# One layer of a hybrid encoder on one Trainium2 core: attention rounds in one piece, full-height neighbourhood scores, w_ple products moved, norms of the end among products, 80 expert blocks ahead

## The chip, the core and the metric

One core of a Trainium2 chip runs the whole layer. TensorE (PE in the profile) multiplies, VectorE (DVE), ScalarE (ACT) and GpSimd (POOL) do the elementwise work, SyncE (SP) issues most DMAs. The metric is the time of one execution on the device in microseconds; the median of three runs is given.

## The reference

A layer over 512 tokens of width 1024, all in float32. An RMS norm and one projection give queries, keys and values of two attentions and two gates. (A) Neighbourhood attention: 8 heads of 64, every token looks at an 8 x 16 window of a grid of 8 rows and 64 columns, with a learned bias. (B) Dilated attention: 12 heads of 64 in three groups with different windows and strides, whose outputs are mixed by their softmax denominators. The outputs are projected, gated, merged and added to x. Then comes a retrieval of experts:

```
q  = rms_norm(x) @ w_query;  s1, s2 = q_halves @ sub_keys        # 128 keys a side, 8 heads
the 16 best of the sums s1 + s2, softmax weights g               # of 128 x 128 experts
x += sum over (head, k) of  gelu(h . expert_u[e]) * g * expert_v[e]
x += sigmoid(rms_norm(x) @ w_ple_gate) * (p @ w_ple)
```

## The kernel before

**Split products.** A float32 weight block is loaded by SP (`wr`), cast to a high part by ScalarE (`wh`, L141) and its rest taken by VectorE (`wl`, L143; letter `v`) or GpSimd (L149; letter `p`). A product is then three matmuls (L171 to L173). The class `Stream` does this in order of `W.add`: three loads ahead, five split blocks at a time; `take` hands blocks to the products and `free` gives their place to the next. Attention scores, transposes and value products are plain float32; a plain float32 product appears as two passes in the trace, a transpose as one.

**Order of work.** Instructions are written in code order, and a scheduler with its own estimate of durations places them on each engine, so the order on TensorE can differ from the code's. `beside` registers filler (a generator of products), and `tick(dt)` lets it go on for the time dt times its rate.

**Stages.** (1) Projections. (2) `pipeline` (L477) runs dilated attention in 24 items of three steps: scores, transposes (`turn`), value products. In each round it calls the scores of one item, the transposes of the item before and the values of the one before that, with a `tick` after each. The filler is the neighbourhood projection. (3) The same for 32 neighbourhood items (a head of a quarter of the tokens each), filler `gates`. A score is one matmul with 64 rows: head h of a pair lies on partitions 0 to 63 or 64 to 127 of `nqk`. (4) Gated branch products (`p`), then w_out (`xo`); after each token tile's second half `norm_parts` (L748) makes the normed tile, transposes it in bank Q and splits it to `hhi`, `hlo`. (5) Query products (`qp`), key scores (`sk`) and the search of the best 16 on VectorE. (6) `ple` twice: pT and w_ple are loaded, 48 matmuls (`pl`), and the results go by 256 columns through a buffer shared with the Gelu outputs (tag `ge`, three deep) to `ple_d` in memory. (7) Ahead: the 128 expert blocks are worked on by whole blocks of `up` (L1008): 24 matmuls `aT`, then a Gelu. For the first NSP = 76 blocks this runs as filler, and the Gelu outputs are stored to `ge_d`. Beside it VectorE builds G, the gate weights of all experts, by one-hot products (`gp`), staged to memory in six parts (`g_d`). One token tile is treated otherwise: its 256 rows of experts are gathered by GpSimd and summed on VectorE (`experts0`). (8) Fused: the 52 later blocks are computed (`up`) and all 128 multiplied with the second expert table (`down`, 18 matmuls `out`); the stored ones are loaded again (`gr`). Four fresh blocks go before the first loaded group. (9) The last `down` products go token tile by token tile, then four norms (`third`), then the w_ple_gate products (`pg`), the gate and the output.

Of the kernel before, what the change touches and what calls it, by code (L numbers as in the profile page):

```python
# [10 lines left out]
F32 = mybir.dt.float32  # L11
# [19 lines left out]

OB = 2

NSP = 76

RATE_LAST, RATE_HEAD, AHEAD = 0.0, 0.1, 1.0
RATE_G, RATE_GATES, EARLY = 1.45, 0.3, 30.0
# [27 lines left out]
def block_kernel(ctx: ExitStack, tc: tile.TileContext, a: dict):  # L65
# [160 lines left out]
    pT = a["pT"].rearrange("(k p) t -> p k t", p=128)  # L226
    for b in range(2):
        add_block(wo, 512 * b, lo="vp")
    for b in range(4):
        add_block(wq, 512 * b, lo="p" if b else "vp")  # L230
    for b in range(2):
        W.add(pT, 2, "p")
        add_block(wpl, 512 * b, lo="p")


    hhi = hpool.tile([128, 8, S], F32R, name="hhi")
# [126 lines left out]
            return qn  # L363
        return second

    def transpose4(src, name="pt"):

        pt = bank("Q", name)
        for c in range(4):
            nc.tensor.transpose(pt[:, 128 * c:128 * c + 128], src[:, 128 * c:128 * c + 128], ident)  # L370
        return pt.rearrange("p (c t) -> p c t", c=4)
# [63 lines left out]
    dils = ExitStack()  # L435
    dilp = dils.enter_context(tc.tile_pool(name="dilp", bufs=1))
    dqk = [dilp.tile([128, 4, 512], F32, name=f"dqk{b}") for b in range(3)]
    dv = [dilp.tile([128, 4, 512], F32, name=f"dv{b}") for b in range(2)]

    dmask = dils.enter_context(tc.tile_pool(name="dmask", bufs=1))  # L440
    m12 = dmask.tile([128, 4, 128], F32, name="m12")
# [35 lines left out]
    def pipeline(items):  # L477

        n = len(items)
        depth = max(len(x) for x in items)  # L480
        for t in range(n + depth - 1):
            for s in range(depth):
                if 0 <= t - s < n and s < len(items[t - s]):
                    tick(items[t - s][s]() or 0.0)


    nas = ExitStack()
    nap = nas.enter_context(tc.tile_pool(name="nap", bufs=1, side="right"))
    nqk = [nap.tile([128, 4, 512], F32, name=f"nqk{s}") for s in range(2)]
    nv = nap.tile([128, 4, 512], F32, name="nv")  # L490

    def na_qk(s):
        def first(i, ps):
            norm = qk_norm(ps, eps_of("j", i))
            box = []

            def third():
                pt = transpose4(box[0].rearrange("p h d -> p (h d)"))
                nc.scalar.activation(nqk[s][:, :, 128 * i:128 * i + 128], pt, AF.Copy, scale=gna[:, s:s + 1])
            return [(3, lambda: box.append(norm())), (7, third)]  # L500
        return first

# [133 lines left out]
    onalo = afix2.tile([128, 4, 512], F32R, name="onalo")  # L636
    gts = ExitStack()
    gt = gts.enter_context(tc.tile_pool(name="gt", bufs=1)).tile([128, 2, 8, 512], F32, name="gt")
    nabs = ExitStack()
    nabp = nabs.enter_context(tc.tile_pool(name="nabp", bufs=1))  # L640

    last_exp = []

# [7 lines left out]
    def na_items(j):  # L651
# [6 lines left out]
        box = {}  # L658

        def bias(hp):  # L660
            t = box["nab", hp] = nabp.tile([128, 2, 256], F32, tag="nab", name="nab", bufs=2)
            nc.sync.dma_start(t, src[:, 2 * hp:2 * hp + 2])

        def item(h):
            p0 = 64 * (h % 2)

            def scores():
                if h == 0:
                    bias(0)
                if h % 2 == 0 and h < 6:  # L670
                    bias(h // 2 + 1)
                sp = bank("P", "sp")[:, :n]
                nc.tensor.matmul(sp, nqk[0][p0:p0 + 64, h // 2, 128 * j:128 * j + 128],
                                 nqk[1][p0:p0 + 64, h // 2, k0:k0 + n], start=True, stop=True)
                sc = box["sc", h] = wk.tile([128, 512], F32, tag="sc", name="sc", bufs=3)[:, :n]
                nc.vector.scalar_tensor_tensor(sc, sp, 0.125, box["nab", h // 2][:, h % 2], op0=ALU.mult, op1=ALU.add)
                nc.vector.tensor_reduce(nm[:, h:h + 1], sc, AX.X, ALU.max, negate=True)
                last_exp[:] = [nc.scalar.activation(sc, sc, AF.Exp, bias=nm[:, h:h + 1],
                                                    accum_out=sums[:, h:h + 1]).ins]
                return n * 4 / 2400  # L680

            def turn():
                pt = bank("Q", "ptp")[:, :n]
                for c in range(nk):
                    nc.tensor.transpose(pt[:, 128 * c:128 * c + 128], box["sc", h][:, 128 * c:128 * c + 128], ident)
                pT = box["pT", h] = wk.tile([128, 512], F32, tag="pT", name="pT", bufs=2)[:, :n]
                nc.scalar.copy(pT, pt)
                return nk * 0.107

            def values():  # L690
                if "uo" not in box:
                    box["uo"] = bank("C", "uo")
                for c in range(nk):
                    nc.tensor.matmul(box["uo"][:, 64 * h:64 * h + 64], box["pT", h][:, 128 * c:128 * c + 128],
                                     vs[c][:, 64 * h:64 * h + 64], start=(c == 0), stop=(c == nk - 1))
                if h == 7:
                    rs = small.tile([128, 8], F32, tag="nrs", name="nrs")
                    nc.vector.reciprocal(rs, sums)
                    o = nabp.tile([128, 8, 64], F32, tag="no", name="no")
                    nc.vector.tensor_mul(o, box["uo"].rearrange("p (h d) -> p h d", h=8),  # L700
                                         col(rs).to_broadcast([128, 8, 64]))

                    def out():
                        pt = transpose4(o.rearrange("p h d -> p (h d)"))
                        oh = onahi[:, :, 128 * j:128 * j + 128]
                        nc.scalar.copy(oh, pt)
                        nc.vector.tensor_sub(onalo[:, :, 128 * j:128 * j + 128], pt, oh.bitcast(F32))
                        return 0.43
                    outs_later.append(out)
                c = nk * 0.107  # L710
                if h == 1:
                    while outs_later:
                        c += outs_later.pop()()
                return c

            return [scores, turn, values]
# [21 lines left out]
    while outs_later:  # L738
        outs_later.pop()()
    done(s)  # L740
    nabs.close()
    nas.close()
    wks.close()

    def square(src, junk, total):
        nc.scalar.activation(junk, src, AF.Square, accum_out=total)

    def norm_parts(src, gain, hn, ssh, cols):  # L748


        ssn = small.tile([128, 1], F32, tag="ssn", name="ssn")
# [3 lines left out]
        for half in range(2):  # L755
            cs = slice(512 * half, 512 * half + 512)
            nc.vector.scalar_tensor_tensor(hn[:, cs], src[:, cs], r, gain[:, cs], op0=ALU.mult, op1=ALU.mult)
            pt = transpose4(hn[:, cs])
            ks = slice(4 * half, 4 * half + 4)
            nc.scalar.copy(hhi[:, ks, cols], pt)  # L760
            nc.vector.tensor_sub(hlo[:, ks, cols], pt, hhi[:, ks, cols].bitcast(F32))
# [52 lines left out]
    for b in range(2):  # L814
        cols = slice(512 * b, 512 * b + 512)
        units = W.take(4)
        for n in range(4):
# [6 lines left out]
            if b:  # L824
                if n:
                    nc.scalar.dma_start(x2_d[n - 1], y)
                hn = x2p.tile([128, D], F32, tag="hn", name="hn", bufs=2) if n else h2n
                norm_parts(y, gffn, hn, ss2[:, n], ts)
    x2s.close()
    gts.close()  # L830
    at.close()
# [88 lines left out]
    def experts0():  # L920
# [16 lines left out]
        for u, (kind, c) in enumerate(units):  # L937
# [13 lines left out]
                    nc.vector.scalar_tensor_tensor(acc0, t, act0[:, c:c + 1], acc0, op0=ALU.mult, op1=ALU.add)  # L951
            yield 1.0

    tiles0 = select_tiles()
    tqs = ExitStack()
    tq = tqs.enter_context(tc.tile_pool(name="tq", bufs=1))
# [25 lines left out]
    later.pop(0)()  # L982

    tqs.close()


    def ple(b):
        (phi, plo), = W.take(1)
        units = W.take(1)
        for n in range(4):  # L990
            ps = bank("P", "pl")
            ts = slice(128 * n, 128 * n + 128)
            run(cell(ps, lambda k: (phi[:, k, ts], plo[:, k, ts]), units, False))
            for c in range(0, 512, 256):
                po = gel.tile([128, 384], F32, tag="ge", name="po", bufs=3)[:, :256]
                nc.scalar.copy(po, ps[:, c:c + 256])
                nc.sync.dma_start(ple_d[128 * n:128 * n + 128, 512 * b + c:512 * b + c + 256], po)
        W.free()
        W.free()

    ple(0)
    ple(1)


    for b in range(NB):
# [20 lines left out]
    k = 0  # L1026
# [145 lines left out]
            run(down(*pend.pop(0), i - 1, V.take(1)))  # L1172
            V.free()

    units = V.take(len(pend))
    for t in range(3):
        for x, p in enumerate(pend):
            run(down(*p, NB - len(pend) + x, units[x:x + 1], [t]))
    done(exp_side)


    fs = ExitStack()
    fin = fs.enter_context(tc.tile_pool(name="fin", bufs=1))
# [6 lines left out]
        with tc.issue_after(late):  # L1190
            nc.sync.dma_start(x3[n], x2_d[n - 1])

    def third(n):
        hn = fin.tile([128, D], F32, tag="hn", name="hn", bufs=2)
        ss3 = small.tile([128, 2], F32, tag="ss3", name="ss3")
        for h in range(2):
# [1 line left out]
            if n:  # L1198
                nc.vector.tensor_add(x3[n][:, cs], x3[n][:, cs], outs[n - 1][h])
            square(x3[n][:, cs], hn[:, cs], ss3[:, h:h + 1])  # L1200
        norm_parts(x3[n], gple, hn, ss3, slice(128 * n, 128 * n + 128))

    for n in (0, 1, 2, 3):
        third(n)
    for b in range(2):
        cols = slice(512 * b, 512 * b + 512)
        units = W.take(4)
        for n in (0, 1, 2, 3):
            ps = bank("A", "pg")
            ts = slice(128 * n, 128 * n + 128)  # L1210
            run(cell(ps, lambda k: (hhi[:, k, ts], hlo[:, k, ts]), units, n == 3))
            pl = fin.tile([128, 512], F32, tag="pl", name="pl", bufs=2)
            with tc.issue_after(late):
                nc.sync.dma_start(pl, ple_d[128 * n:128 * n + 128, cols])
            sg_ = fin.tile([128, 512], F32, tag="sg", name="sg", bufs=1)
            nc.scalar.activation(sg_, ps, AF.Sigmoid)
            nc.vector.tensor_mul(pl, sg_, pl)
            nc.vector.tensor_add(pl, pl, x3[n][:, cols])
            nc.sync.dma_start(a["out"][128 * n:128 * n + 128, cols], pl)
    fs.close()  # L1220
    dns.close()
    gps.close()
# [66 lines left out]
```

## Time and profile before

| | |
|---|---|
| median of three runs | 1806.03 us (1803.46 to 1808.21) |
| the profiled execution | 1807.68 us, its span 1805.7 us |
| TensorE busy | 1774.1 us |
| VectorE / ScalarE / GpSimd busy | 1314.0 / 727.4 / 525.8 us |
| DMA | 417.11 MB, 231 GB/s in the mean |

Busy time is the union of an engine's instructions. A matmul's busy time contains its filling and draining, which overlap with its neighbours, so a fully busy TensorE can still be slower than its work needs: the distance between the starts of matmuls tells that. "Idle before" names what the engine waited for.

### The profile page before, as it was taken

What the parts mean: (1) busy time and instruction counts of PE and PEld (TensorE: products, weight loads), DVE (VectorE), ACT (ScalarE), POOL (GpSimd) and SP (SyncE); (2) the same over time, 40 slices, a digit from 0 to 9 for tenths busy, and PEclk for the clock granted to TensorE, in tenths of its full rate; (3) what the DMA queues carried; (4) which work ended last, traced back from release to release, by engine and by line L of the source; (5) the groups of instructions that cost most, each with busy time, mean ns of one, the idle gap of its engine ahead of it and who ended that gap; (6) DMA issues with size and microseconds to landing.
All of it is one profiled execution on the core that took longest, in us unless ns stands there. A gap on an engine that the chain in (4) does not pass through costs nothing.

```text
span 1805.7 us, 26185 instructions
## 1 busy us (share of the span) xinstructions
PE 1774.1 (98%) x9613; PEld 1561.1 (86%) x9613; DVE 1314.0 (73%) x2638; ACT 727.4 (40%) x1202; POOL 525.8 (29%) x428
## 2 busy tenths in 40 slices
PE   8999999999899899999999999999999999999998
PEld 7997777788788799999999988888888888888877
DVE  6634644436568899998989578787878878776864
ACT  5434554443323544444444433333333333333342
POOL 4201101113424121223354134343334323333300
PEclk9999999999999999999999999999999999999999
DMA  5231114334312576688888999999999989989922
GB/s 189 77 93 34 47 52 124 96 110 139 118 59 94 164 257 207 242 285 316 305 321 325 365 320 350 341 335 339 342 325 343 351 317 356 343 313 317 347 97 82
DMA packets 159536, 417.11 MB, mean 231 GB/s; under 512 B 14128, under 2 KB 61488, under 8 KB 156336
## 3 DMA queue, kind: packets, MB, share of 16 engines
q1 hardware_dynamic: 122112, 279.64, 44.4%
q0 software_dynamic: 36864, 134.23, 20.8%
q8 instruction: 75, 1.23, 0.3%
q10 hardware_dynamic: 432, 1.57, 0.2%
q14 instruction: 53, 0.43, 0.1%
HBM read 368.73 MB, written 45.88 MB: 230 GB/s over the span
## 4 chain that ended last, share of the span: by engine, by line
PE 91%; DMA 4%; DVE 2%; ACT 1%; issue 1%; SPq 0%; POOL 0%; ACTq 0%; DVEq 0%; POOLq 0%
PE out L1153 27%; PE aT L171 9%; PE aT L173 9%; PE aT L172 9%; PE proj L171 3%; PE proj L172 3%; PE proj L173 3%; PE gp L1103 3%; DMA g_d<-stage 2%; PE gt L173 2%; PE gt L171 2%; PE gt L172 2%; DMA vr<-peer_expert_v 2%; PE qp L171 2%; PE qp L172 2%; PE qp L173 2%
## 5 line engine op out<-in xcount | busy, mean ns | idle before, releaser
L171 PE MATMUL aT<-hhi,wh 128*128 128x384 f32 x1024 | 345.4, 337 | 4.0 <-ACT ge L1020 4.0
L173 PE MATMUL aT<-hhi,wl 128*128 128x384 f32 x1024 | 344.9, 337 | 0.0
L172 PE MATMUL aT<-hlo,wh 128*128 128x384 f32 x1024 | 344.7, 337 | 0.0
L141 ACT CAST wh<-wr 128x1024 fp32r<-128x1024 f32 x216 | 226.8, 1052 | 263.7 <-PE aT L172 194.1
L143 DVE TENSOR_TENSOR wl<-wr,wh 128x1024 fp32r<-128x1024 f32 x184 | 229.0, 1245 | 124.4 <-ACT wh L141 122.9
L932 POOL DMA_INDIRECT gath<-peer_expert_u,eidx x128 | 181.4, 1417 | 435.9 <-DVE gath L943 296.9
L932 POOL DMA_INDIRECT gath<-peer_expert_v,eidx x128 | 191.4, 1495 | 302.3 <-DVE acc L951 213.5
L1153 PE MATMUL out<-vl,ahi 128*128 128x512 f32 x768 | 237.2, 390 | 0.0
L1153 PE MATMUL out<-vh,ahi 128*128 128x512 f32 x768 | 233.0, 391 | 2.4 <-ACT ahi L1141 2.4
L1153 PE MATMUL out<-vh,alo 128*128 128x512 f32 x768 | 233.7, 390 | 0.0
L141 ACT CAST vh<-vr 128x1024 fp32r<-128x1024 f32 x128 | 134.4, 1051 | 178.3 <-DMA vr<-peer_expert_v 156.3
L171 PEld LDWEIGHTS aT<-hhi,wh 128*128 128x128 f32 x1024 | 192.8, 188 | 7.0 <-ACT ge L1020 4.4
L172 PEld LDWEIGHTS aT<-hlo,wh 128*128 128x128 f32 x1024 | 192.9, 188 | 2.3
L173 PEld LDWEIGHTS aT<-hhi,wl 128*128 128x128 f32 x1024 | 192.9, 188 | 1.0
L951 DVE SCALAR_TENSOR_TENSOR acc<-gath,act,acc 128x1024 f32<-128x1024 f32 x128 | 164.0, 1281 | 34.6 <-DMA gath<-peer_expert_v,eidx 34.2
L143 DVE TENSOR_TENSOR vl<-vr,vh 128x1024 fp32r<-128x1024 f32 x128 | 156.1, 1222 | 36.4 <-ACT vh L141 35.1
L149 POOL TENSOR_TENSOR wl<-wr,wh 128x256 fp32r<-128x256 f32 x128 | 99.4, 813 | 250.5 <-ACT wh L141 220.8
L1153 PEld LDWEIGHTS out<-vl,ahi 128*128 128x128 f32 x768 | 144.1, 188 | 31.0 <-DVE vl L143 0.2
L1153 PEld LDWEIGHTS out<-vh,alo 128*128 128x128 f32 x768 | 144.0, 188 | 31.0 <-DVE alo L1143 0.7
L943 DVE SCALAR_TENSOR_TENSOR gath<-gath,h2n 128x1024 f32<-128x1024 f32 x128 | 155.6, 1222 | 20.2 <-DMA gath<-peer_expert_u,eidx 20.0
L1153 PEld LDWEIGHTS out<-vh,ahi 128*128 128x128 f32 x768 | 143.0, 188 | 29.4 <-ACT ahi L1141 3.5
L171 PE MATMUL proj<-wh,hhi 128*128 128x512 f32 (+1 forms) x256 | 108.1, 425 | 6.8 <-ACT wh L141 6.8
(259 smaller groups left out, 2849.2 us busy)
## 6 DMA issues: line engine op xcount, KB each, us to landing
vr<-peer_expert_v SPq DMA_DIRECT2D x128, 512.0 KB
wr<-uT SPq DMA_DIRECT2D x128, 512.0 KB
g_d<-stage SPq DMA_DIRECT2D x24, 1024.0 KB
G<-g_d SPq DMA_DIRECT2D x32, 768.0 KB
wr<-w_in SPq DMA_DIRECT2D x46, 512.0 KB
ge_d<-ge SPq DMA_DIRECT2D x76, 192.0 KB
gr<-ge_d SPq DMA_DIRECT2D x76, 192.0 KB
wr<-peer_w_query SPq DMA_DIRECT2D x16, 512.0 KB
```

Source lines behind the costliest of these rows:

```text
L141: nc.scalar.copy(hi, self.raw[i])
L143: nc.vector.tensor_sub(lo, self.raw[i], hi.bitcast(F32))
L149: nc.gpsimd.tensor_sub(l[:, cs], r[:, cs], h[:, cs].bitcast(F32))
L171: nc.tensor.matmul(ps, st[0], mv[0], start=start, stop=False)
L172: nc.tensor.matmul(ps, st[0], mv[1], start=False, stop=False)
L173: nc.tensor.matmul(ps, st[1], mv[0], start=False, stop=stop)
L932: nc.gpsimd.indirect_dma_start(out=t, out_offset=None, in_=a["peer_expert_" + kind], in_offset=bass.IndirectOffsetOnAxis(ap=eidx[:, c:c + ...
L943: nc.vector.scalar_tensor_tensor(t, t, 1.0, h2n, op0=ALU.mult, op1=ALU.mult, accum_out=a0[:, c:c + 1])
L951: nc.vector.scalar_tensor_tensor(acc0, t, act0[:, c:c + 1], acc0, op0=ALU.mult, op1=ALU.add)
L1103: nc.tensor.matmul(gpb[:, 128 * x:128 * x + 128], o[:, 1, cs], m[:, s, cs], start=(s == 0), stop=(s == 2))
L1153: nc.tensor.matmul(outs[t][h], w[:, cs], x[:, h], start=first and p == 0, stop=last and p == 2)
```

## The change

NSP goes from 76 to 80. `pipeline` calls the three steps of a round and then one `tick` with their sum. Neighbourhood queries are stored by parity of the head into a tensor whose other 64 rows are zero, so that a score multiplies all 128 rows. The bias tiles and outputs of that attention use buffers of the pool `wk`. w_ple products are queued and computed before the query products, and pT is loaded once. `norm_parts` becomes a generator that stops between the normed tile and its transposes; at the end, norms start between the last `down` products, with a bank of their own each, and the transposes stand between the w_ple_gate products, which are in a function `gated` now.

```diff
-NSP = 76
+NSP = 80
...
+    W.add(pT, 2)
+    for b in range(2):
+        add_block(wpl, 512 * b)
     for b in range(4):
         add_block(wq, 512 * b, lo="p" if b else "vp")
-    for b in range(2):
-        W.add(pT, 2, "p")
-        add_block(wpl, 512 * b, lo="p")
...
         for t in range(n + depth - 1):
+            dt = 0.0
             for s in range(depth):
                 if 0 <= t - s < n and s < len(items[t - s]):
-                    tick(items[t - s][s]() or 0.0)
+                    dt += items[t - s][s]() or 0.0
+            tick(dt)
...
-    nqk = [nap.tile([128, 4, 512], F32, name=f"nqk{s}") for s in range(2)]
+    nqz = nap.tile([128, 4, 2, 512], F32, name="nqz")
+    nkk = nap.tile([128, 4, 512], F32, name="nkk")
+    for par in range(2):
+        nc.gpsimd.memset(nqz[64 - 64 * par:128 - 64 * par, :, par], 0.0)
...
-                nc.scalar.activation(nqk[s][:, :, 128 * i:128 * i + 128], pt, AF.Copy, scale=gna[:, s:s + 1])
+                cols = slice(128 * i, 128 * i + 128)
+                if s:
+                    nc.scalar.activation(nkk[:, :, cols], pt, AF.Copy, scale=gna[:, 1:2])
+                    return
+                for par in range(2):
+                    rows = slice(64 * par, 64 * par + 64)
+                    nc.scalar.activation(nqz[rows, :, par, cols], pt[rows], AF.Copy, scale=gna[rows, 0:1])
...
-                nc.tensor.matmul(sp, nqk[0][p0:p0 + 64, h // 2, 128 * j:128 * j + 128],
-                                 nqk[1][p0:p0 + 64, h // 2, k0:k0 + n], start=True, stop=True)
+                nc.tensor.matmul(sp, nqz[:, h // 2, h % 2, 128 * j:128 * j + 128], nkk[:, h // 2, k0:k0 + n],
+                                 start=True, stop=True)
...
-            pt = transpose4(hn[:, cs])
+        yield
+        for half in range(2):
+            pt = transpose4(hn[:, 512 * half:512 * half + 512], tag=tag)
             ks = slice(4 * half, 4 * half + 4)
...
+    (phi, plo), = W.take(1)
+    for b in range(2):
+        units = W.take(1)
+        for n in range(4):
+            ps = bank("P", "pl")
+            ts = slice(128 * n, 128 * n + 128)
+            run(cell(ps, lambda k: (phi[:, k, ts], plo[:, k, ts]), units, False))
+            for c in range(0, 512, 256):
+                po = gel.tile([128, 384], F32, tag="ge", name="po", bufs=3)[:, :256]
+                nc.scalar.copy(po, ps[:, c:c + 256])
+                nc.sync.dma_start(ple_d[128 * n:128 * n + 128, 512 * b + c:512 * b + c + 256], po)
+    for _ in range(3):
+        W.free()
     tiles0 = select_tiles()
...
-    ple(0)
-    ple(1)
...
-    for n in (0, 1, 2, 3):
-        third(n)
+    norms = {}
+    def norm(n):
+        if n in norms:
+            for _ in norms[n]:
+                pass
+            return
         hn = fin.tile([128, D], F32, tag="hn", name="hn", bufs=2)
...
+        norms[n] = norm_parts(x3[n], gple, hn, ss3, slice(128 * n, 128 * n + 128), "APQC"[n])
+        next(norms[n])
...
+    done(exp_side)
+    norm(0)
+    units = V.take(len(pend))
+    for t in range(3):
+        for x, p in enumerate(pend):
+            run(down(*p, NB - len(pend) + x, units[x:x + 1], [t]))
+        if t == 0:
+            norm(0)
+        if t < 2:
+            norm(t + 1)
+    units = W.take(4)
+    gated(0, 0, units)
+    norm(1)
+    norm(3)
+    gated(0, 1, units)
+    norm(2)
+    gated(0, 2, units)
+    norm(3)
+    gated(0, 3, units)
+    units = W.take(4)
+    for n in range(4):
+        gated(1, n, units)
```

## Rows read from the trace of the kernel before

**Rows 1.** The page's first part: busy us, share of the span, instructions.
```profile
PE 1774.1 (98%) x9613; PEld 1561.1 (86%) x9613; DVE 1314.0 (73%) x2638; ACT 727.4 (40%) x1202; POOL 525.8 (29%) x428
```

**Rows 2.** Busy time by stretch: us, engines, granted clock, DMA share, GB/s.
```profile
45.00:480.00 435.00, 434.44 (x2109) 356.65 (x2109) 214.57 (x493) 183.34 (x394) 77.30 (x75) 1.00 0.28 87
595.00:630.00 35.00, 30.10 (x149) 26.70 (x148) 31.54 (x168) 19.58 (x35) 7.01 (x11) 0.95 0.66 207
630.00:1005.00 375.00, 372.77 (x2914) 366.09 (x2913) 342.31 (x578) 172.21 (x278) 118.58 (x58) 1.00 0.79 282
1025.00:1600.00 575.00, 575.00 (x2738) 501.73 (x2737) 462.72 (x608) 210.37 (x288) 214.15 (x168) 1.00 0.95 339
1600.00:1665.00 65.00, 63.10 (x304) 54.82 (x303) 44.92 (x51) 20.58 (x29) 22.78 (x17) 1.00 0.90 318
```

**Rows 3.** Waits of TensorE: us in total, times, longest us.
```profile
PE pt L370 <- DVE hn L757: 4.1, 1, 4.1
PE aT L171 <- ACT ge L1020: 4.0, 1, 4.0
...
PE out L1153 <- ACT ahi L1141: 2.4, 3, 1.1
```

**Rows 4.** Timeline of TensorE in neighbourhood attention: start us, us, instruction.
```profile
297.32 0.39 PE L685 MATMUL ptp<-ident,sc 128*128 128x128 f32 x2
297.64 0.70 PE L673 MATMUL sp<-nqk,nqk 64*128 64x256 f32 x2
298.27 0.50 PE L173 MATMUL gt<-hhi,wl 128*128 128x512 f32 x1
298.61 0.39 PE L171 MATMUL gt<-hhi,wh 128*128 128x512 f32 x1
298.84 0.39 PE L172 MATMUL gt<-hlo,wh 128*128 128x512 f32 x1
```

**Rows 5.** Timeline of TensorE at the sums of squares of the start.
```profile
21.56 0.39 PE L173 MATMUL proj<-wh,hlo 128*128 128x512 f32 x1
21.79 1.88 PE L390 MATMUL ssb<-xsq,ones 128*128 128x512 f32 x4
...
23.97 0.40 PE L172 MATMUL proj<-wl,hhi 128*128 128x512 f32 x1
```

**Rows 6.** Timeline of TensorE where two neighbourhood scores stand together.
```profile
330.60 0.70 PE L673 MATMUL sp<-nqk,nqk 64*128 64x256 f32 x4
...
331.80 0.40 PE L173 MATMUL gt<-hhi,wl 128*128 128x512 f32 x1
```

**Rows 7.** ScalarE's timeline, one exponential's end; then two groups of splits.
```profile
299.78 0.19 ACT L678 ACTIVATION_READ_ACCUMULATOR sc<-sc,nnm 128x1 f32 x1
...
L141 ACT CAST wh<-wr 128x1024 fp32r<-128x1024 f32 x216 | 226.8, 1052 | 263.7 <-PE aT L172 194.1
...
L143 DVE TENSOR_TENSOR wl<-wr,wh 128x1024 fp32r<-128x1024 f32 x79 | 96.6, 1224 | 16.4 <-ACT wh L141 15.8 <-issue 0.6
```

**Rows 8.** Timeline of TensorE from the last w_out product to steady query products.
```profile
485.18 1.03 PE L370 MATMUL pt<-ident,hn 128*128 128x128 f32 x8
...
498.18 0.39 PE L173 MATMUL qp<-hhi,wl 128*128 128x512 f32 x1
```

**Rows 9.** Timeline of the w_ple results: a store's issue, a later copy.
```profile
601.35 1.30 SPq L997 DMA_DIRECT2D ple_d<-po  x3
...
603.81 0.37 ACT L996 COPY po<-pl 128x256 f32<-128x256 f32 x1 [1.93 <-DMA ple_d<-po]
```

**Rows 10.** SP's timeline: the last writes of G and its first load.
```profile
1000.58 3.64 SPq L1112 DMA_DIRECT2D g_d<-stage  x4
...
1012.50 1.28 SPq L1133 DMA_DIRECT2D G<-g_d  x2
```

**Rows 11.** Timeline of TensorE at the end's first norms.
```profile
1750.86 1.03 PE L370 MATMUL pt<-ident,hn 128*128 128x128 f32 x8
...
1754.83 0.39 PE L171 MATMUL pg<-wh,hhi 128*128 128x512 f32 x1
```

More of the change, by code (lines that the diff above doesn't have):

```diff
@@ L364, in qk_norm, with transpose4 @@
         return second
-    def transpose4(src, name="pt"):
-        pt = bank("Q", name)
+    def transpose4(src, name="pt", tag="Q"):
+        pt = bank(tag, name)
         for c in range(4):
@@ L437, in block_kernel @@
     dqk = [dilp.tile([128, 4, 512], F32, name=f"dqk{b}") for b in range(3)]
-    dv = [dilp.tile([128, 4, 512], F32, name=f"dv{b}") for b in range(2)]
+    dv = [dilp.tile([128, 4, w], F32, name=f"dv{w}") for w in (512, 256)]
     dmask = dils.enter_context(tc.tile_pool(name="dmask", bufs=1))
@@ L660, in bias @@
         def bias(hp):
-            t = box["nab", hp] = nabp.tile([128, 2, 256], F32, tag="nab", name="nab", bufs=2)
+            t = box["nab", hp] = wk.tile([128, 2, 256], F32, tag="q", name="nab", bufs=2)
             nc.sync.dma_start(t, src[:, 2 * hp:2 * hp + 2])
         def item(h):
-            p0 = 64 * (h % 2)
             def scores():
@@ L698, in values @@
                     nc.vector.reciprocal(rs, sums)
-                    o = nabp.tile([128, 8, 64], F32, tag="no", name="no")
+                    o = wk.tile([128, 8, 64], F32, tag="sq", name="no", bufs=1)
                     nc.vector.tensor_mul(o, box["uo"].rearrange("p (h d) -> p h d", h=8),
@@ L740, in block_kernel @@
     done(s)
-    nabs.close()
     nas.close()
@@ L746, in square, with norm_parts @@
         nc.scalar.activation(junk, src, AF.Square, accum_out=total)
-    def norm_parts(src, gain, hn, ssh, cols):
+    def norm_parts(src, gain, hn, ssh, cols, tag="Q"):
         ssn = small.tile([128, 1], F32, tag="ssn", name="ssn")
@@ L827, in block_kernel @@
                 hn = x2p.tile([128, D], F32, tag="hn", name="hn", bufs=2) if n else h2n
-                norm_parts(y, gffn, hn, ss2[:, n], ts)
+                for _ in norm_parts(y, gffn, hn, ss2[:, n], ts):
+                    pass
     x2s.close()
@@ L984, in block_kernel @@
     tqs.close()
[L987 to L999, printed above, removed]
-    ple(0)
-    ple(1)
     for b in range(NB):
@@ L1173, in block_kernel @@
             V.free()
[L1175 to L1179, printed above, removed]
     fs = ExitStack()
@@ L1191, in block_kernel @@
             nc.sync.dma_start(x3[n], x2_d[n - 1])
-    def third(n):
+    norms = {}
+    def norm(n):
+        if n in norms:
+            for _ in norms[n]:
+                pass
+            return
         hn = fin.tile([128, D], F32, tag="hn", name="hn", bufs=2)
@@ L1200, in third, with gated @@
             square(x3[n][:, cs], hn[:, cs], ss3[:, h:h + 1])
-        norm_parts(x3[n], gple, hn, ss3, slice(128 * n, 128 * n + 128))
-    for n in (0, 1, 2, 3):
-        third(n)
-    for b in range(2):
+        norms[n] = norm_parts(x3[n], gple, hn, ss3, slice(128 * n, 128 * n + 128), "APQC"[n])
+        next(norms[n])
+    def gated(b, n, units):
         cols = slice(512 * b, 512 * b + 512)
[L1207 to L1219, printed above, removed]
+        ps = bank("A", "pg")
+        ts = slice(128 * n, 128 * n + 128)
+        run(cell(ps, lambda k: (hhi[:, k, ts], hlo[:, k, ts]), units, n == 3))
+        pl = fin.tile([128, 512], F32, tag="pl", name="pl", bufs=2)
+        with tc.issue_after(late):
+            nc.sync.dma_start(pl, ple_d[128 * n:128 * n + 128, cols])
+        sg_ = fin.tile([128, 512], F32, tag="sg", name="sg", bufs=1)
+        nc.scalar.activation(sg_, ps, AF.Sigmoid)
+        nc.vector.tensor_mul(pl, sg_, pl)
+        nc.vector.tensor_add(pl, pl, x3[n][:, cols])
+        nc.sync.dma_start(a["out"][128 * n:128 * n + 128, cols], pl)
+    done(exp_side)
[20 more added lines that the diff above has]
+        gated(1, n, units)
     fs.close()
```

2 lines of the change are left out of this document (removed).

## The prediction

> **What bounds the kernel now.** I read the page's first part, then busy time by stretch, the waits of TensorE, and last the timeline, start to start. TensorE is busy 98% of the span and idle for only 31.6 us [rows 1]; VectorE has 73%. From 45 to 480 us it lacks 0.6 us of 435, and from 1025 to 1600 nothing [rows 2]. So time can only come from its few stalls, or from products that hold it longer than their work. A matmul's busy time overlaps the next one's, so a price is read as the distance between starts: 0.23 us for a 512-column product of the split weights.
>
> The stalls have names [rows 3]: 4.1 us on the last norm before the queries, 4.0 us on the first Gelu of the expert stage, 2.4 us on `ahi` when G arrives late. The hidden price is in the scores. Between 297.32 and 298.84 [rows 4] stand two transposes, one 64-high score (two passes) and two gate products: 1.52 us. A full-height product in the same two passes exists: four passes of 512 columns and two projections take 21.79 to 23.97, 2.18 us [rows 5], which is 4 x 0.43 + 2 x 0.23 with nothing over, and it begins 0.23 us after the product before it. At that rate 256 columns are 0.21 us a pass, and the first stretch should be 2 x 0.11 + 2 x 0.21 + 2 x 0.23 = 1.11. The lone 64-high score pays 0.41 us too much.
>
> **The change, part by part.** The sum is made against the profiled execution, 1807.7 us (span 1805.7 and 2.0 around it); the median of the runs is 1.7 lower.
>
> *Full-height scores.* There are 32 scores of two passes. On the timeline 26 stand alone, at 0.34 to 0.42 too much each, and three times two stand together. In such a pair four passes take no longer than two elsewhere: 330.60 to 331.80 [rows 6] is 1.20, as is 297.64 to 298.84 [rows 4], so a pair costs what two full-height scores would. Gain 26 x 0.40 = 10.4. The trace has no full-height 256-column score; bounds are 0 and 26 x 0.42 = 10.9, and I take the upper, since rows 5 are the same two-pass product with other columns. Four more ScalarE copies and the zeroing on GpSimd lie in a stretch where those engines are busy 183 and 77 of 435 us [rows 2]; without that cover they would delay a norm, which waits seven steps of 1.4 us for its transposes anyway. Bias tiles and outputs in other pools: same DMAs, nothing.
>
> The TensorEngine Tiling page of the Trainium skill (Theoretical Speedup) says that a contraction of 64 can run up to twice as fast in two halves of the array, which speaks against filling the height with zeros. The pair of rows 6 agrees in its inner passes, the lone score of rows 4 doesn't. By the rule applied to all 32, this part would gain nothing and the sum would come to about 1796.
>
> *Rounds back to back.* The dilated scores stay 64 high. Now a round's scores are followed by transposes instead of a split-weight product. The exit into such a product costs 0.11 (298.27 to 298.61 is 0.34, not 0.23 [rows 4]); into transposes between 0 and that. Half, in 24 rounds: 1.3, bounds 0 and 2.6. Added wait: behind a transpose stand the value products and the filler, in order. It needs the exponential of the round before. That chain ends 1.7 us after the score's end (298.27 [rows 4] to 299.97 [rows 7]); a new neighbourhood round is 0.43 + 0.22 + 0.45 + filler 1.33 (credit 0.86 x 1.45, in units of 1.28 credits that take 6 x 0.23) = 2.4 us. So no wait, unless a weight's cast and split (1.05 us on ScalarE, 1.22 on VectorE [rows 7]) fall into the chain.
>
> *w_ple products ahead of the queries.* Between 485.18 and 498.18 [rows 8] TensorE has 24 transposes (2.6 us) and six query products (1.4 us): 9.0 of 13.0 us are lost to the last norms and the load of the query weights, the slow first products included. 48 w_ple products (48 x 0.23 = 10.9 us) come to stand there; their inputs come behind the w_out blocks on SP, one of two loads of pT falls away, and their splits go from GpSimd to VectorE (three of 1.22). Their 16 stores are queued on SP among the loads of the query weights, which are asked for three ahead. They aren't free cover: their results leave through three buffers, and from a store's issue to the next copy it is 2.5 us [rows 9], about 2.85 us for three with the copy. 16 halves need 15.2 us, transposes and products 13.5: 1.7 us late. ScalarE holds those copies in order ahead of the last norm's casts and of the third query unit's split. I leave 2.5 us lost, between 0 and the old 9.0: gain 6.5.
>
> *What they leave behind.* From 595 to 630 us 4.9 us are idle and the granted clock is 0.95 [rows 2], 1.7 us more: 6.7 lost. The Gelu output shares its three buffers with the w_ple results, so it waited for their stores. Without them I leave 1.0 lost. What is late next is G. The distance from the last key product (598.3) to the first value product (1025.1) is set by both sides: TensorE loses 10.9 + 5.7 us there and gets four more blocks, 4 x 24 x 0.173 = 16.6 us, so it comes to G at the same time as now. G is just in time today: its last writes are issued at 1000.58, its load at 1012.50 [rows 10], and TensorE already waits for `ahi` [rows 3]. VectorE builds it, 342 of 375 us busy [rows 2], and gets four more splits of 1.22 us before G's end, because TensorE takes weights sooner: 4.9 us. It has 33 us of gaps, so I take half, 2.5, between 0 and 4.9. Net gain of this part 6.7 - 1.0 - 2.5 = 3.2.
>
> The row 595 to 630, with its idle time, shows 0.95 granted in the mean, so part of it ran at the lower of the two clocks, 1.2 GHz. TensorE: Matmul & The Clock Gate (Part 1: The HAM clock gate) says that low activity throttles the clock and activity releases it, so a new wait at G brings a slow stretch with it. By that rule the wait costs up to 1.7 us more and the forecast would be 1787. But the short waits from 1600 to 1665 left the clock at 1.00 [rows 2], so I leave it out.
>
> *80 blocks ahead.* Four blocks (16.6 us) leave the fused stage and stand before it, as counted above: no TensorE work saved. Their Gelu outputs go out and come back, 1.6 MB, on SP. The fused stage moves 339 GB/s at a DMA share of 0.95 [rows 2] and shortens by 16.6 of 726 us while its bytes fall by half a percent: share 0.97. There were already 1.9 us idle at 1600 to 1665. I take 2.0 lost, between 0 and 13 (share stuck at 0.95).
>
> *Norms of the end.* From 1750.86 to 1754.83 [rows 11] there are 12 transposes and three products, 2.0 of 4.0 us. Now norms start after each token tile's last products and transposes get banks of their own; w_ple_gate products cover the others. Gain 1.8, bounds 0 and 2.0. The tail behind the last product stays.
>
> Sum: 10.4 + 1.3 + 6.5 + 3.2 - 2.0 + 1.8 = 21.2. 1807.7 - 21.2 = 1786.5, as a median 1785.
>
> **Rivals.**
> - *G late by all 4.9 us, with a slow stretch of 1.7:* 2.4 + 1.7 more, 1789. For: VectorE's 91% while it builds G. Against: its gaps. 0.14.
> - *The fused stage is bound by DMA:* 11 more, 1796. For: 0.95, and stretches of loaded blocks that need more than the fused ones. Against: it gave no wait until 1600. 0.13.
> - *Better:* products hide the norms wholly, G and DMA cost nothing: 2.5 + 2.5 + 2.0 and 1.3 from the rounds, 1777. 0.14.
> - *The tiling rule holds for lone scores:* 1796. Rows 4 to 6 are against it. 0.02.
> - *It doesn't do what it says:* the order on TensorE isn't the code's, the scheduler places instructions by its own estimate; if it puts the last transposes ahead of the w_ple products, 6.5 is gone: 1792. 0.03.
> - *Slower:* rounds meet splits. With a cast and a split in it the chain is 4.0 us against a round of 2.4. At half of that wait, 0.8 us in each of 34 rounds, 27 us are lost: 1812. It decides from 0.6 us a round. Against: no wait of TensorE between 90 and 400 us today. 0.05.
>
> **How the numbers follow.** The forecast has 0.49, its own range 1779 to 1791. The range 1772 to 1799 takes in all but the slower case and parts of the DMA and better ones. This measurement tells 0.3% (5.4 us) from no change. Faster is all below 1800.6: 0.90; no change, the worse end of the DMA case, 0.05; slower 0.05.
>
> **What would show it.** Right: neighbourhood scores 128 high, 1.1 us in the stretch of rows 4; no wait on `hn` before the queries, and a clock of 1.00 there; no wait on the first Gelu; transposes of the end without waits. Wrong: TensorE waiting in the attention rounds, over 6 us idle before the first value product, or more than 5 us idle in the fused stage.

## The result, and the profile after

The changed kernel takes 1786.92 us (median of 4 runs, 1785.56 to 1787.83) against 1806.24 us before (4 runs): a ratio of 0.9894, with a 95% interval of 0.9876 to 0.9911. The medians lie 19.3 us apart. The profiled execution has a span of 1783.3 us, 22.4 less than before; this pair, from which the stage figures of these two kernels come, differs by 3.1 us more than the medians do.

The views of the changed kernel answer to those of before. First the page's opening part:

```profile
PE 1758.6 (99%) x9613; PEld 1561.3 (88%) x9613; DVE 1320.6 (74%) x2641; ACT 730.3 (41%) x1206; POOL 504.9 (28%) x414
```

TensorE runs as many instructions as before, 9613 [rows 1], is busy 15.5 us less for them and idle 24.7 us instead of 31.6. So most of the gain is not idle time: products hold the engine less long. A part of it is the clock: the kernel before ran from 490.96 to 497.80 us at a granted clock of 0.50 (1.2 GHz), in and behind the waits on the norms ahead of the queries, and from 624.0 to 627.5 at 0.51, behind the wait on the first Gelu. The changed kernel has one such stretch, at 966.6 to 970.0 (below).

Busy time by stretch, columns as in [rows 2]:

```profile
595.00:630.00 35.00, 35.00 (x207) 35.00 (x206) 35.00 (x182) 17.57 (x26) 0.00 (x0) 1.00 0.57 186
630.00:1005.00 375.00, 372.18 (x2906) 366.50 (x2905) 338.75 (x555) 171.70 (x275) 107.24 (x58) 1.00 0.80 283
1025.00:1600.00 575.00, 572.48 (x2709) 496.81 (x2709) 462.69 (x607) 207.11 (x284) 213.35 (x167) 1.00 0.94 338
```

The stretch from 595 to 630, which lost 4.9 us of idle time and had a granted clock of 0.95 [rows 2], is now full and at 1.00. The stretch to 1005 is as full as it was. From 1025 to 1600, in the fused stage, 2.5 us are lacking where nothing lacked.

The waits of TensorE:

```profile
PE proj L171 <- ACT wh L141: 6.8, 1, 6.8
PE pl L171 <- ACT po L975: 3.3, 2, 2.6
PE gp L1111 <- ACT stage L1114: 2.8, 2, 2.2
PE proj L172 <- DVE wl L143: 1.9, 1, 1.9
PE out L1161 <- DVE alo L1151: 1.5, 1, 1.5
...
PE out L1161 <- ACT ahi L1149: 0.7, 2, 0.5
```

The waits on `hn` and on the Gelu output `ge` [rows 3] are gone. Grown are those on `po`, the copies of the w_ple results, to 3.3 us, and those on the mask copies `stage`, to 2.8 us (0.9 and 1.3 before). Behind the longer of these, TensorE's timeline and its busy time show the slow stretch:

```profile
966.79 4.36 PE L1111 MATMUL gp<-m,o 128*128 128x128 bf16 x48 [2.25 <-ACT stage L1114]
970.96 0.42 PE L173 MATMUL aT<-hhi,wl 128*128 128x384 f32 x1
```

```profile
966.60:970.00 3.40, 3.21 (x31) 3.21 (x31) 0.45 (x1) 2.06 (x6) 0.00 (x0) 0.50 1.02 408
```

From start to start the 48 mask products take 4.17 us, where 48 x 0.056 are 2.7. Last, the timeline of a neighbourhood score between gate products:

```profile
272.43 0.59 PE L682 MATMUL sp<-nkk,nqz 128*128 128x256 f32 x2
272.67 0.59 PE L171 MATMUL gt<-hhi,wh 128*128 128x512 f32 x1
273.10 0.40 PE L172 MATMUL gt<-hlo,wh 128*128 128x512 f32 x1
273.33 0.40 PE L173 MATMUL gt<-hhi,wl 128*128 128x512 f32 x1
```

Starts 272.43 to 273.33 are 0.90 us for two passes of 256 columns and two products: 2 x 0.21 + 2 x 0.23 = 0.88. The lone score of [rows 4] paid 0.4 more.

**The loss of TensorE by stage.** The table is worked out from the starts on TensorE's timelines: what the distance from one start to the next has beyond the undisturbed one of its kind (0.227 us for a product of 512 columns, 0.173 for one of 384, 0.11 for a transpose or value product, 0.43 for 512 columns of a score's pass, 0.056 for a mask product), summed over a stage. Records missing from a trace count as loss, so 1 us of a long stage means nothing. The last three columns are the way from the last mask product to the first value product, the fused stage, and the end from the last value product on.

| kernel | start | dilated | neighb. | w_out to keys | keys to masks | masks | to values | fused | end |
|---|---|---|---|---|---|---|---|---|---|
| before | 11.6 | 13.4 | 9.6 | 9.0 | 8.0 | 6.8 | 0.2 | 8.1 | 2.1 |
| changed | 10.8 | 12.1 | 0.1 | 4.5 | 0.6 | 8.2 | 0.9 | 8.5 | 0.9 |
| scores at half height | 13.7 | 12.2 | 9.5 | 5.8 | 0.6 | 6.9 | 0.2 | 11.1 | 0.9 |
| w_ple behind the queries | 10.7 | 12.1 | 0.1 | 10.7 | 9.9 | 4.4 | 0.2 | 13.4 | 0.6 |
| before + full height | 13.8 | 13.1 | 0.1 | 8.4 | 8.6 | 4.0 | 0.2 | 9.6 | 2.1 |
| + dilated at full height | 13.4 | 5.8 | 0.1 | 4.4 | 0.6 | 6.5 | 0.9 | 11.4 | 0.9 |
| + six buffers for w_ple | 9.7 | 12.1 | 0.1 | 1.8 | 3.1 | 7.8 | 0.2 | 9.6 | 0.9 |
| both of these | 10.8 | 5.8 | 0.1 | 1.8 | 0.6 | 6.2 | 1.3 | 7.1 | 0.9 |

The start was not touched and still moves by 4 us from kernel to kernel, and the fused stage by several.

### The profile page after: what moved, and what is told of

It is laid out like the page before. It is cut to its first block, busy times and chain, and to the rows that moved or that the text cites. A ratio compares the mean times of both kernels' runs of the same rounds, so it can differ in the third digit from the quotient of the medians.

```text
span 1783.3 us, 26229 instructions
## 1 busy us (share of the span) xinstructions
PE 1758.6 (99%) x9613; PEld 1561.3 (88%) x9613; DVE 1320.6 (74%) x2641; ACT 730.3 (41%) x1206; POOL 504.9 (28%) x414
## 4 chain that ended last, share of the span: by engine, by line
PE 89%; DMA 6%; DVE 3%; issue 1%; ACT 1%; SPq 0%; ACTq 0%; DVEq 0%
PE out L1161 27%; PE aT L171 8%; PE aT L173 8%; PE aT L172 8%; PE proj L171 3%; PE proj L172 3%; PE proj L173 3%; PE gp L1111 3%; DMA g_d<-stage 3%; DMA vr<-peer_expert_v 2%; PE gt L171 2%; PE gt L173 2%; PE gt L172 2%; PE qp L171 2%; PE qp L172 2%; PE qp L173 2%
## 5 line engine op out<-in xcount | busy, mean ns | idle before, releaser
L943 POOL DMA_INDIRECT gath<-peer_expert_u,eidx x128 | 175.9, 1374 | 472.7 <-DVE gath L954 327.9
L943 POOL DMA_INDIRECT gath<-peer_expert_v,eidx x128 | 183.8, 1436 | 309.6 <-DVE acc L962 227.3
L1161 PE MATMUL out<-vh,ahi 128*128 128x512 f32 x768 | 224.3, 391 | 1.5 <-ACT vh L141 0.9
L149 POOL TENSOR_TENSOR wl<-wr,wh 128x256 fp32r<-128x256 f32 x112 | 86.3, 809 | 234.9 <-ACT wh L141 195.3
## 6 DMA issues: line engine op xcount, KB each, us to landing
g_d<-stage SPq DMA_DIRECT2D x24, 1024.0 KB, 11.6
```

What stands on the lines that cost most here:

```text
L149: nc.gpsimd.tensor_sub(l[:, cs], r[:, cs], h[:, cs].bitcast(F32))
L943: nc.gpsimd.indirect_dma_start(out=t, out_offset=None, in_=a["peer_expert_" + kind], in_offset=bass.IndirectOffsetOnAxis(ap=eidx[:, c:c + ...
L1161: nc.tensor.matmul(outs[t][h], w[:, cs], x[:, h], start=first and p == 0, stop=last and p == 2)
```

## The experiments

Diffs are against the changed kernel, where nothing else is said. Each kernel computes the whole layer. The kernel before was run again beside each of them, with medians from 1805.45 to 1808.20 us, so the ratios compare better than the times; a distance "by ratio" is the difference of two ratios times 1806 us.

### Scores of the neighbourhood at half height again

```diff
-                nc.tensor.matmul(sp, nqz[:, h // 2, h % 2, 128 * j:128 * j + 128], nkk[:, h // 2, k0:k0 + n],
+                p0 = 64 * (h % 2)
+                nc.tensor.matmul(sp, nqz[p0:p0 + 64, h // 2, h % 2, 128 * j:128 * j + 128], nkk[p0:p0 + 64, h // 2, k0:k0 + n],
```

> The changed kernel with one thing undone: a neighbourhood score multiplies only the 64 rows of its head again. Theory (a lone 64-high score holds TensorE 0.40 us too long on its way in, between its passes and on its way out): 26 to 32 lone scores, 10 to 12 us more than the changed kernel's 1787, 1798. Rival (64-high products run up to twice as fast, the height brings nothing): 1787 or less. Rival (the gain came from the rounds in one piece): under 3 us more.

Measured: 1800.15 us, ratio to before 0.9955 (0.9939 to 0.9972), 13.2 us above the changed kernel (11.0 by ratio); 1798 was expected. The timeline of TensorE in this kernel:

```profile
273.46 0.40 PE L173 MATMUL proj<-wh,hlo 128*128 128x512 f32 x1
273.78 0.70 PE L683 MATMUL sp<-nkk,nqz 64*128 64x256 f32 x2
274.41 0.50 PE L171 MATMUL gt<-hhi,wh 128*128 128x512 f32 x1
274.74 0.40 PE L172 MATMUL gt<-hlo,wh 128*128 128x512 f32 x1
274.98 0.40 PE L173 MATMUL gt<-hhi,wl 128*128 128x512 f32 x1
```

Entry 0.32 instead of 0.23, two passes 0.63 instead of 0.43, exit 0.33 instead of 0.23: 0.4 us too much for one lone score, with the same tiles, copies and zeroes in place. So the price comes with the height, not with the layout. The stage's loss goes back from 0.1 to 9.5 us. The rest of the 13.2 stands in this profile at the start (2.9 more) and in the fused stage (2.6 more), with smaller differences of both signs.

The Trainium skill says on the page TensorEngine Tiling (Array Packing), under Key Properties, that a change of the tiling mode drains TensorE. The entry and exit of the lone score in these rows agree with it, at about 0.1 us each. It does not say why the two passes themselves take 0.2 us longer, and no run here shows that.

### Full-height scores alone, in the kernel before

The edit is the change's tiles `nqz` and `nkk` and its score product put into the kernel before, whose rounds, order and 76 blocks stay; bias tiles and outputs go to other pools to make room.

> The kernel before with the full-height neighbourhood scores alone (and the bias tiles and outputs in the pool of the attention's work tiles, to make room). Theory: 10 us less than before, 1796. Rival (the stages behind take it back, as G is waited for): 1803 or more.

Measured: 1799.14 us, ratio 0.996 (0.9948 to 0.9973); 1796 was expected, 3 us less. The neighbourhood stage loses 0.1 instead of 9.6 us, and TensorE does not wait in it. Of these 9.5 us the span shows 8.7 (1797.0 against 1805.7) and the medians 7.1; start and fused stage lost 3.7 more in this profile, the masks 2.8 less.

### One tick of the filler after every step

```diff
-                    dt += items[t - s][s]() or 0.0
-            tick(dt)
+                    tick(items[t - s][s]() or 0.0)
```

> The changed kernel with a tick after each step of a round again, full-height scores kept. Theory (a round in one piece saves half of a 64-high score's way out, in the dilated rounds alone): 1 to 2 us more, 1788. Rival (rounds in one piece are what quickened attention): 5 to 10 more, 1793 or above.

Measured: 1789.27 us, ratio 0.9917 (0.9902 to 0.9931). The dilated stage loses 13.1 us against 12.1, the neighbourhood stage 0.1 in both. The spans of the two profiles are 1782.7 and 1783.3: the gain of the rounds is about 1 us in one stage, too small for the times to show. TensorE does not wait in the attention rounds of either; the rival of rounds that meet splits is out.

### w_ple behind the queries, 80 blocks kept

```diff
+    for b in range(4):
+        add_block(wq, 512 * b, lo="p" if b else "vp")
     W.add(pT, 2)
     for b in range(2):
         add_block(wpl, 512 * b)
-    for b in range(4):
-        add_block(wq, 512 * b, lo="p" if b else "vp")
...
```

The loop of w_ple products moves from ahead of `tiles0 = select_tiles()` to behind the last key products, unchanged.

> The changed kernel with the w_ple products behind the queries again (their loads too; pT still once; 80 blocks ahead). Theory: TensorE loses 9 us at the norms ahead of the queries instead of 4.8 and again 6 to 7 us around the first Gelus, whose buffers the w_ple results share: 10 to 11 more, 1798. Rival (the move only changes who fills which gap, the time is set by when G is ready): about 4 more, 1791.

Measured: 1803.66 us, ratio 0.9981 (0.9966 to 0.9996), 16.7 us above the changed kernel (15.7 by ratio); 1798 was expected. The waits of TensorE in it:

```profile
PE aT L171 <- ACT ge L1029: 7.3, 1, 7.3
PE proj L171 <- ACT wh L141: 7.0, 1, 7.0
PE pt L370 <- DVE hn L765: 4.6, 1, 4.6
PE pt L370 <- DVE hlo L771: 2.4, 1, 2.4
```

and its busy time from the last products of w_out to past the queries:

```profile
480.00:630.00 150.00, 139.83 (x691) 121.30 (x692) 122.94 (x730) 56.92 (x91) 34.36 (x48) 0.95 0.33 107
```

The waits on `hn`, `hlo` and `ge` are back, 10.2 us idle, and the granted clock of the stretch is 0.95. By stage the loss is 6.2 us more ahead of the queries and 9.3 more behind the keys, the masks give 3.8 back, and the fused stage loses 4.9 more, which was not in the expectation and is not told from its scatter. So the move of w_ple is worth both stalls, and the second one more than the first.

### 76 blocks ahead

```diff
-NSP = 80
+NSP = 76
```

> The changed kernel with 76 blocks ahead instead of 80. Theory (G's building on VectorE sets when the value products can begin; the four blocks only fill the time until then): TensorE idles 13 to 17 us ahead of the first value product, 1801. Rival (G isn't what is waited for; moving blocks moves no TensorE work): 1787, or a little less for less traffic.

Measured: 1824.1 us, ratio 1.0089 (1.0064 to 1.0114): slower than before, 37 us above the changed kernel (35 by ratio), and 23 us beyond what was expected. The chain of waits in this kernel (start us, us, what):

```profile
998.30 12.57 DMA g_d<-stage
...
1011.33 5.15 DMA G<-g_d
...
1016.50 0.57 DVE ge L1147
...
1017.09 0.52 ACT ahi L1149
...
1017.65 0.79 PE out L1161
```

The waits of TensorE, busy time, and the timeline at the first value products:

```profile
PE out L1161 <- ACT ahi L1149: 22.5, 8, 14.7
...
PE out L1161 <- DVE vl L143: 4.7, 7, 1.2
...
PE out L1161 <- ACT vh L141: 3.1, 4, 1.6
```

```profile
995.00:1035.00 40.00, 25.30 (x116) 21.87 (x116) 23.34 (x35) 12.18 (x16) 7.51 (x6) 0.83 0.93 343
1035.00:1200.00 165.00, 162.85 (x777) 141.65 (x776) 128.07 (x163) 58.99 (x81) 56.04 (x46) 1.00 0.91 326
1200.00:1400.00 200.00, 192.54 (x903) 164.46 (x902) 150.02 (x200) 67.11 (x93) 71.68 (x56) 1.00 0.90 316
```

```profile
1017.65 1.22 PE L1161 MATMUL out<-vh,ahi 128*128 128x512 f32 x2 [14.70 <-ACT ahi L1149]
1018.67 1.05 PE L1161 MATMUL out<-vl,ahi 128*128 128x512 f32 x2
...
1021.63 0.62 PE L1161 MATMUL out<-vl,ahi 128*128 128x512 f32 x2
```

From the last writes of G to its first load's end lie 18 us, and TensorE has nothing to do in 14.7 of them: the four blocks (16.6 us) were the cover. That part of the expectation is shown, and after the stall the first two products take 1.02 us from start to start instead of twice 0.23: the granted clock is 0.50 from 1007.4 to 1021.05, 0.83 in the mean of the row's 40 us. What was not expected comes later: 2.2 us idle to 1200 and 7.5 to 1400, where the changed kernel has none, at a DMA share of 0.90. It is not the 76 blocks as such: the kernel before and the one with the full-height scores alone have as many, come to G without a stall, and lose 8.1 and 9.6 us in the fused stage. So the extra waits go with the stall at the entry; that it causes them is argued and not shown. By which way it could (value loads waiting on SP behind the loads of G and of the gates, or gathers that run ahead) was not settled.

### 84 blocks ahead

```diff
-NSP = 80
+NSP = 84
```

> The changed kernel with 84 blocks of gates ahead instead of 80. The fused stage's DMA share is 0.94 to 0.95 at 338 to 342 GB/s, so theory: the 16.6 us of products that move ahead of the first output product are not gained, because the gathers and value loads of the fused stage can't be moved faster: that stage stays at 703 to 710 us and loses 8 to 16 us in waits for values, and the time is 1796 us (1791 to 1803). Rival 1, that TensorE bounds the stage: it gets shorter by 16.6 us (694), the stretch ahead of it longer by as much, and the time is that of the changed kernel, 1787 us. Rival 2, that the 2.8 us of waits for the mask copies and the 0.9 us before the first output product come from too few blocks ahead: 1784 us.

Measured: 1793.84 us, ratio 0.9918 (0.9901 to 0.9935). The fused stage takes 710.2 us from first to last value product, as in the changed kernel, the stretch ahead of it 31.8 instead of 25.6. So the theory's time holds. Rival 1's 694 us and rival 2's 1784 us don't, though the interval overlaps a little with that of the changed kernel. But the edit did not do what it was meant to: the stretch ahead grew by 6.2 us only, not 16.6. Counted in the traces, TensorE has done the 24 `aT` products of 85.0 blocks ahead of the first value product in the changed kernel and of 86.7 here. So 1.7 of the four blocks moved, about 7 us of products, and the others stayed in the fused stage. The theory's reason isn't shown either:

```profile
1200.00:1400.00 200.00, 197.85 (x931) 170.45 (x930) 163.89 (x218) 73.74 (x102) 81.64 (x59) 1.00 0.95 344
...
1600.00:1730.00 130.00, 126.69 (x579) 106.50 (x578) 98.82 (x114) 44.07 (x60) 49.73 (x33) 0.99 0.91 321
```

TensorE idles 2.2 and 3.3 us in these two stretches, at DMA shares of 0.95 and 0.91. The kernel before ran at 0.95 from 1025 to 1600 without idling [rows 2], so the share alone does not set the wait. The longest waits in the two stretches are 1.6 us on `ahi` and 2.4 on `vh`; why these come late was not settled.

### The old end

The four norms stand together again, ahead of the w_ple_gate products, with one bank for their transposes.

```diff
-        norms[n] = norm_parts(x3[n], gple, hn, ss3, slice(128 * n, 128 * n + 128), "APQC"[n])
+        norms[n] = norm_parts(x3[n], gple, hn, ss3, slice(128 * n, 128 * n + 128), "Q")
...
+    done(exp_side)
+    for n in range(4):
+        norm(n)
+        norm(n)
...
```

> The changed kernel with the end as before: all value products, then the four norms with transposes in one pair of banks, then the gate products. Theory: 2 us more idle between the last value product and steady gate products, 1789. Rival (products hide the norms anyway): 1787.

Measured: 1788.79 us, ratio 0.9887 (0.9867 to 0.9907). The interval does not tell it from the changed kernel. In the trace the end, from the last value product on, takes 49.0 us against 47.1, the 2 us expected.

### The wide dilated scores at full height

The same step for the 16 dilated score groups that are 512 columns wide (heads 0 to 3):

```diff
-    dqk = [dilp.tile([128, 4, 512], F32, name=f"dqk{b}") for b in range(3)]
+    dqk = dilp.tile([128, 10, 512], F32, name="dqk")
+    dqz = dilp.tile([128, 2, 2, 512], F32, name="dqz")
+    for par in range(2):
+        nc.gpsimd.memset(dqz[64 - 64 * par:128 - 64 * par, :, par], 0.0)
...
+        if head < 4:
+            return dqz[:, head // 2, head % 2, 128 * i:128 * i + 128]
...
```

> The changed kernel with the 16 dilated scores of whole sequences (heads 0 to 3) at full height as well. Theory: a lone 64-high score costs 0.35 to 0.40 whatever it multiplies, 16 of them 5.6 to 6.4 us, 1781. Rival (in a round in one piece they cost little): under 2 us less.

Measured: 1783.22 us, ratio 0.9885 (0.9862 to 0.9907). The dilated stage takes 169.7 us instead of 176.0: 6.3 us, 0.39 a score, where 5.6 to 6.4 were expected. The group of these scores (busy us, mean ns), first in the changed kernel, then in this one:

```profile
L538 PE MATMUL sp<-dqk,dqk 64*128 64x512 f32 x32 | 18.0, 641 | 0.0
```

```profile
L551 PE MATMUL sp<-dqk,dqz 128*128 128x512 f32 x32 | 16.3, 591 | 0.0
```

The busy time alone shows 1.7 of the 6.3 us: it overlaps with its neighbours, and only starts tell the price. The time of the whole kernel does not show it: the median is 3.7 us lower (1.6 by ratio) where 1781 was expected, and the interval overlaps that of the changed kernel. In this profile the start and the fused stage lost 5.5 us more.

### Own buffers for the w_ple results

```diff
+    plp = pls.enter_context(tc.tile_pool(name="plp", bufs=1))
...
-                po = gel.tile([128, 384], F32, tag="ge", name="po", bufs=3)[:, :256]
+                po = plp.tile([128, 256], F32, tag="po", name="po", bufs=6)
```

> The changed kernel with six buffers of their own for the w_ple results instead of three that they share. Theory: the 3.3 us that TensorE waits for their copies at 480 us go, 1784. Rival (the last norms are what is late there, the wait only shows itself at another instruction): 1786 or more.

Measured: 1786.22 us, ratio 0.9895 (0.9873 to 0.9918): no change; 1784 was expected, and the rival's 1786 is what came. Waits of TensorE in this kernel:

```profile
PE gp L1114 <- ACT stage L1117: 4.0, 2, 2.8
PE out L1164 <- ACT vh L141: 2.0, 1, 2.0
PE ipt L1086 <- DVE best L778: 1.7, 1, 1.7
PE pl L171 <- ACT po L977: 0.8, 1, 0.8
```

The wait on `po` falls from 3.3 to 0.8 us, so the three buffers were its cause, and not the last norms, as the rival had it. What is saved there, 2.7 us by stage, is lost again behind the keys, 2.5, of which 1.7 us are a wait on the selection tables (`best`) of VectorE, to which TensorE now comes earlier.

### Both of these

> The 16 wide dilated scores at full height (worth 6.3 us in their own stage before) and six buffers of their own for the w_ple results, together. Theory, that what the six buffers save ahead of the queries is waited for again later, at the weight conversions: no better than the full-height dilated scores alone, 1783 us (1781 to 1786), with some 2 us of waits before the first query product and some 3 more after the last key product than in the changed kernel. Rival, that the two gains add up: 1780 us or less.

Measured: 1777.79 us, ratio 0.9852 (0.9834 to 0.9871), an interval just below that of the changed kernel; I had expected 1781 to 1786, the rival 1780 or less. The interval still overlaps a little with that of the full-height dilated scores alone (0.9862 to 0.9907), so the time nearly decides against my theory that the buffers' gain is given back. The stages do decide in this trace: ahead of the queries and behind the keys 2.4 us are lost, with the dilated scores alone 5.0. This version has the lowest median. Its first part of the page and its waits:

```profile
PE 1750.2 (99%) x9613; PEld 1562.1 (88%) x9613; DVE 1318.6 (74%) x2641; ACT 730.9 (41%) x1210; POOL 516.2 (29%) x416
```

```profile
PE gp L1127 <- ACT stage L1130: 2.2, 2, 1.5
...
PE out L1177 <- ACT vh L141: 1.4, 1, 1.4
PE pl L171 <- ACT po L990: 1.2, 1, 1.2
```

The waits on `best` and `ge` don't appear. Why TensorE, 9 us earlier at the selection than in the changed kernel, finds the tables ready here and not with the buffers alone, I have not found out. The profiled execution was its fastest run, 1773.7 us.

## Why the prediction was right

The forecast was 1785 us, the time 1786.92, and the mechanism is the one it gave; that the sum comes out so near is in part luck, as the steps show. By its steps (predicted, then measured by the table above):

- **Full-height scores, 10.4: 9.5.** Shown from both sides, by taking the height away from the changed kernel and giving it alone to the kernel before. The price read from [rows 4] as a distance between starts was 0.40 us for a lone score; the 26 cost 0.37 each. The wide dilated scores repeat it at 0.39 us each. What the Trainium skill gives on the page TensorEngine Tiling (Array Packing), under Theoretical Speedup, up to twice the speed for a contraction of 64, shows in the pairs of [rows 6], four passes in the time of two, and not in lone scores.
- **Rounds back to back, 1.3: 1.3,** of which the experiment with the ticks gives 1.0 back. Too small for the times.
- **w_ple ahead of the queries, 6.5: 4.5.** This term was mis-sized. [Rows 9] gave 1.7 us for copies that wait for a buffer; it is 3.3. ScalarE's timeline of the changed kernel shows why:

```profile
480.05 0.58 ACT L770 CAST hhi<-pt 128x512 fp32r<-128x512 f32 x1 [1.92 <-PE pt L370]
482.66 0.37 ACT L975 COPY po<-pl 128x256 f32<-128x256 f32 x1 [2.02 <-DMA ple_d<-po]
482.93 0.59 ACT L770 CAST hhi<-pt 128x512 fp32r<-128x512 f32 x1
```

  A copy stands 2.02 us on a store, the next norm's cast behind it in order, and TensorE waits 2.63 us for the copy, until 483.08. I had spread the shortage evenly over the 16 halves; it falls at one point, where ScalarE's queue also holds the norm. Six buffers take 2.5 of the 3.3 us away.
- **What they leave behind, 3.2: 5.3.** Ahead of the masks 8.0 us of loss became 0.6; I had 6.7 to 1.0, because the waits on `ge` and the slow clock were counted and the small waits around them weren't. Against that, 0.7 us more are lost at the first value product, where G comes late, and 1.4 more at the masks, 2.1 where I took 2.5 for G alone. The 1.4 are not G: the stretch at a granted clock of 0.50 behind the mask wait costs 1.5 (above). So the slow stretch that I left out did come, at another wait. I had also misread [rows 3]: of the 2.4 us on `ahi` in the kernel before, 1.9 lie between 1600 and 1665 and 0.5 at 1730, none at the first value product; there the first `ahi` was done at 1024.39 and used at 1025.14, so G had 0.7 us to spare. SP's timeline, to be read beside [rows 10]:

```profile
995.99 3.67 SPq L1120 DMA_DIRECT2D g_d<-stage  x4
1010.95 0.99 SPq L1141 DMA_DIRECT2D G<-g_d  x2
```

  The last writes go 4.6 us earlier than before, the load only 1.6: in the chain of waits the last write takes until 1010.9 to land, 12.2 us, and the load's issue follows it.
- **80 blocks ahead, -2.0: -0.4** in the fused stage, within its scatter. The working counted the four blocks as cover for G in the step before and only their cost here. The experiment shows what that cover is worth: without it the change is slower than the kernel before (1824.1 us).
- **Norms of the end, 1.8: 1.2,** in one trace; the times don't show it.

These are 21.4 us of 21.2 predicted, and the span's other 1.0 comes from the rest: the untouched start lost 0.8 less. The errors, -2.0 and +2.1 at w_ple and behind it, cancel, and so nearly do those of the scores, the blocks and the end (-0.9, +1.6 and -0.6). That is luck as far as is shown: the experiment with the six buffers exchanges a wait at one stall for one at the next, the one with both changes does not. And the sum is that of the profiled pair; the medians give 19.3.

Of the rivals, G late by 4.9 us, the fused stage at its DMA bound and rounds that wait for splits did not occur. The first is what happens with 76 blocks, three times as large. Of the signs that were named, no wait on `hn`, a clock of 1.00 ahead of the queries and no wait on the first Gelu are there, and the transposes of the end wait for nothing; a gate product waits 0.3 us.

## What to carry to other kernels

Price a product by the distance between starts, not by its busy time: the lone 64-high scores cost 0.4 us too much each in a profile that shows TensorE busy 98%. When a stretch of cover is moved, ask at the next late input (here G) who covers it now, and change both in one step: either half alone was slower than the pair, by 16.7 and 37 us. Look for a gain at one stall at the next one too: with six buffers alone 2.7 us were gained and 2.5 lost again behind it, with both changes they were kept.

## What the runs showed that I had not expected

- The kernel with a stall of 14.7 us at the head of the fused stage lost more than the stall. It has 26.4 us more idle time of TensorE than the changed one and 9.9 more busy time for the same 9613 instructions (1768.5 against 1758.6), with a granted clock of 0.50 (1.2 GHz) from 1007.4 to 1021.05, in and behind the stall, and 0.92 in the first 45 us, which the edit does not touch. The Trainium skill, TensorE: Matmul & The Clock Gate (Part 1: The HAM clock gate), has low activity throttle the clock; the 0.50 here agrees with it.
- A short wait can have a slow stretch behind it, and need not: 2.25 us on `stage` in the changed kernel have a granted clock of 0.50 (1.2 GHz) behind them, until 970.0, and 2.6 us on `po` ahead of the queries have 1.00. What decides it was not tested.
- The first 45 us run at a granted clock of 0.92 to 1.00 in kernels whose start is the same, and the loss of the start goes with it: 9.7 to 10.8 us at 1.00, 13.4 to 13.8 at 0.92. One profile is no measure of a gain of that size; the stage in which the edit lies is.
